# Splitting modulated tokens into two 12-bit parts once per tile and layer, and loading the parts

## The chip, the core and the metric

The kernel runs on one core of a Trainium2 chip. Its time is the device time of one execution in microseconds (us). Names: PE is the matrix engine (TensorE), ACT ScalarE, DVE VectorE, POOL GpSimd, SP the engine that issues most transfers; `L339` is line 339 of the kernel before. A tile is 128 tokens; there are 18 (16 of the latent grid, 2 of the context).

## The reference

Two layers of a hybrid block on 2048 latent tokens and 256 context tokens, 1024 features, fp32. In each layer all head groups read the same modulated input through one projection:

```python
h = x * (1.0 + scale[:, None]) + shift[:, None]          # and hc = ctx * (1 + scale_c) + shift_c
(aq, ak, av, ag, bq, bk, bv, bg, cq, ck, cv, cg, du, dg) = jnp.split(h @ w_in, IN_SPLITS, axis=-1)
ya = gqa(aq, ak, av)          # group A: 4 heads, 2 key heads, rms-normed q and k, rotary
yb = diff_attention(bq, bk, bv)   # group B: 4 heads, two softmax maps each
yc = neighbourhood(cq, ck, cv)    # group C: 4 heads, 8 x 16 window plus the context keys
yd = s5(du)                       # group D: state-space layer over the tokens
y = concat(ya * silu(ag), yb * silu(bg), yc * silu(cg), yd * silu(dg)) @ w_out
x = layer_norm(ALPHA * x + gate * y)
```

`w_in` has 3328 columns, so `h @ w_in` is done here in parts: eleven passes ("sweeps") over the 18 tiles in each layer, each for the columns of one unit of work.

## The kernel before

*Products in two parts.* A product of fp32 numbers is made of three products of numbers with 12-bit mantissas (type fp32r, which PE takes at full rate): the tile h is split into H and L, the weights into WH and WL, and `mm3k` adds H WH + H WL + L WH for each of the 8 feature tiles, 24 matmuls a tile of tokens. H is a copy of h into fp32r by ACT (L337), L = h - H by POOL (L339), or, where `solo` is set, a quarter by POOL and three quarters by DVE (L340).

*Where the split stands.* The modulated tokens of a layer lie in DRAM (`hT`, 512 KB a tile). Every sweep loads each tile from there (`load_h`, L390, issued by SP) and splits it again (`split`). In the first layer the first sweep, that of group D, makes h from the input (`modulate`) and stores it; for the second layer the output projection of the first does so in `late`, for one tile while the products of the next are made.

*Stages of a layer.* The sweep of group D's input; the state-space scan; a sweep for A's first unit together with group D's gates; then the chain of ten attention units, a0 b0 a1 b1 c0 b2 c1 b3 c2 c3, which takes most of the time; the output projection. The two first sweeps run by themselves (`sweep`). The other nine units' sweeps run beside the attention of units before them (`sweep_beside`), as five streams of pieces: `pe` (matmuls, a feature tile a piece), `act` and `dve` (what is done with the product), `load` (load and split), `keys` (transposes of keys). `attend_a` and `attend` are written out by hand: they call `F.pe`, `F.act`, `F.dve` at fixed places, and these emit the next piece of a stream whose condition holds. `load` goes two tiles ahead (`("mm", j - 2) in at`). `F.light` says whether the DVE may take a share of L; it is set in C units.

*What sets the order.* In the chain, PE, ACT and DVE run in the order in which the program emits. POOL's and SP's orders are laid out by a scheduler. Every engine works off its instructions in order, so one that waits holds what is queued behind it.

*In a B unit* a step has the scores of one map (L998), their maxima (L1042), the exponentials (L1057), the combination of two maps on DVE (L1081, 1024 and 1280 columns), transposes (L1097) and products with values (L1123). The sweep of a C unit beside it splits the keys on DVE (L736, L737). In an A unit DVE finds maxima (L810) and DVE and POOL add up sums (L894).

The lines about the split:

```python
def split(self, h, solo, later=None):
    H = self.hp.tile([128, NK, 128], F32R, name="hH", bufs=2)
    L = self.hp.tile([128, NK, 128], F32R, name="hL", bufs=2)
    nc.scalar.activation(H, h, AF.Copy)
    a = 2 if solo else NK
    nc.gpsimd.tensor_tensor(L[:, :a], h[:, :a], H[:, :a], op=OP.subtract)
```

Of the kernel before, what the change touches and what calls it, by code (L numbers as in the profile page):

```python
# [35 lines left out]
AHEAD = 8  # L36
A_HEAD = 1
# [19 lines left out]
class Beside:  # L57
    """Streams of pieces of work that run beside attention: a projection's products, what ScalarE and VectorE do
    with them, the operands, and the keys' transposes. A stream yields None after a piece, and a condition
    where the next piece needs another stream's."""  # L60
    def __init__(self, prev, per):
        self.prev, self.per, self.sub = prev, per, []
# [20 lines left out]
class Fill:  # L83
    """Projections beside attention, one after another: plan names them, and what makes their streams."""
    def __init__(self, plan):
        self.plan, self.made, self.last, self.freed = list(plan), {}, None, set()
        self.q, self.t, self.light, self.draining, self.merged = [], 0, False, False, False
# [10 lines left out]
    def release(self, name):  # L98
        """The place for a projection's results is free."""
# [16 lines left out]
    def dve(self):  # L116
        for s in self.q[:2]:
            while s.sub:
                s.sub.pop(0)()
# [32 lines left out]
    def ahead(self, name, n):  # L152
        """The first steps of the first projection."""
# [7 lines left out]
class Net:  # L161
# [9 lines left out]
    # ------------------------------------------------------------------ set-up  # L171
    def consts(self):
# [32 lines left out]
        self.hT = {(l, t): dr.tile([128, NK, 128], F32, name=f"hT{l}_{t}") for l in range(DEPTH) for t in range(NT)}  # L205
# [6 lines left out]
    def stage(self):  # L212
        """Six banks of PSUM for one stage of the work."""
# [22 lines left out]
    def ada_w(self, l, c, j, p, bufs):  # L236
        """Two feature tiles of 512 columns of the modulation's weights."""
        w = p.tile([128, 2, 512], F32, name="hT", bufs=bufs)
# [22 lines left out]
    def ada(self, l, p):  # L261
        """Shift and scale, features on partitions."""
# [8 lines left out]
    def ada_beside(self, prev, F, chunks):  # L271
        """The same in pieces that run beside attention, for chunks of a layer's columns each."""
# [4 lines left out]
        def fetch(i):  # L277
            if i < len(jobs):
                c, j = jobs[i]
                ws[i] = self.ada_w(*chunks[c], j, self.hp, 2)  # L280

        def pe():
            yield lambda: S.prev is None or S.prev.read
            fetch(0)
            fetch(1)
            for i, (c, j) in enumerate(jobs):
# [4 lines left out]
                for k in (2 * j, 2 * j + 1):  # L291
# [3 lines left out]
                    if k % 2:  # L295
                        fetch(i + 2)
                    yield None

        def act():
            for c in range(len(chunks)):  # L300
                yield lambda: c in pss and (c < 1 or c - 1 in done)
                rows[c] = self.ada_row(pss.pop(c), self.hp.tile([2, 512], F32, name="hH", bufs=2))
# [1697 lines left out]
```

## Time and profile before

| | before |
|---|---|
| time, median of 3 runs | 5335.41 us (5329.9 to 5342.77) |
| span of the profiled execution | 5332.0 us (no other time of it is shown) |
| PE busy | 4758.8 us, 89% |
| DVE busy | 3709.5 us, 70% |
| ACT busy | 2903.1 us, 54% |
| POOL busy | 2474.4 us, 46% |
| moved by DMA | 460.67 MB, mean 86 GB/s |
| mean granted PE clock | 0.953 |

Busy time is the union of an engine's instructions; matmuls are pipelined and their ends are modelled, so a busy PE can still have short waits inside. A wait is put down to the instruction whose end released it. The granted clock is a share of full speed (1.0 is 2.4 GHz, 0.5 is 1.2 GHz). Stretches used below: 70 to 196 us group D's sweep of the first layer, 2805 to 2891 us that of the second; 4017 to 4228 us unit b1 of the second layer; six C units (c0, c1, c2 of both layers).

### The profile page before, as it was taken

The page shows a single profiled execution, that of the slowest core. Times are in us where ns is not written, and L with a number is a line of the kernel's source. Part 1 is how long each engine was busy: PE and PEld are TensorE (multiplying, and loading weights), DVE is VectorE, ACT ScalarE, POOL GpSimd, SP SyncE. Part 2 cuts the span into 40 slices and gives each one's busy share as a digit, 9 for nine tenths or more (in the row PEclk, how much of TensorE's full clock was granted, in tenths as well). Part 3 has the DMA queues.
Part 4 walks back from the last instruction along what each step waited for, and adds up shares of the span by engine and source line. Part 5 has one row for each costly group of instructions (what it writes and reads, how often), then busy time and mean ns, then how long its engine had stood idle before and what let it go on. Part 6 is the DMA issues. An engine that isn't in the chain of part 4 may idle for free. (4 is left out here: it accounts for less than half of the span.)

```text
span 5332.0 us, 87066 instructions
## 1 busy us (share of the span) xinstructions
PE 4758.8 (89%) x31076; PEld 3619.3 (68%) x31076; DVE 3709.5 (70%) x7186; ACT 2903.1 (54%) x6882; POOL 2474.4 (46%) x3017
## 2 busy tenths in 40 slices
PE   7878988899899998998997889988998989989999
PEld 3776546665678777775677765476656777867777
DVE  8575758876785966933974847697768759578345
ACT  3432437644676876854333434476447768667541
POOL 5355544645445354441533745546554544544322
PEclk8999999999999999999998999999999989989999
DMA  7734101111113122134556261112111221221333
GB/s 246 213 110 129 40 27 36 60 44 34 53 55 93 51 75 72 46 106 125 179 185 189 92 169 45 32 36 59 44 42 52 60 83 47 82 63 52 96 120 114
DMA packets 360193, 460.67 MB, mean 86 GB/s; under 512 B 161872, under 2 KB 262224, under 8 KB 359760
## 3 DMA queue, kind: packets, MB, share of 16 engines
q1 hardware_dynamic: 353712, 449.80, 27.7%
q8 instruction: 246, 4.03, 0.3%
q10 hardware_dynamic: 6048, 5.31, 0.3%
q14 instruction: 187, 1.53, 0.1%
HBM read 363.48 MB, written 91.49 MB: 85 GB/s over the span
## 5 line engine op out<-in xcount | busy, mean ns | idle before, releaser
L339 POOL TENSOR_TENSOR hL<-hT,hH 128x1024 fp32r<-128x1024 f32 (+1 forms) x396 | 822.7, 2079 | 897.9 <-ACT hH L337 705.6
L380 PE MATMUL pj<-WH,hH 128*128 128x256 f32 (+2 forms) x2592 | 825.8, 319 | 11.5 <-ACT b_v L729 2.9
L382 PE MATMUL pj<-WH,hL 128*128 128x256 f32 (+2 forms) x2592 | 765.0, 295 | 32.1 <-POOL hL L339 32.1
L381 PE MATMUL pj<-WL,hH 128*128 128x256 f32 (+2 forms) x2592 | 761.5, 294 | 0.0
L380 PEld LDWEIGHTS pj<-WH,hH 128*128 128x128 f32 x2592 | 506.8, 196 | 121.4 <-issue 72.3
L1111 ACT ACTIVATE PT<-tr 128x512 f32<-128x512 f32 (+1 forms) x788 | 440.2, 559 | 209.4 <-PE tr L1097 200.6
L382 PEld LDWEIGHTS pj<-WH,hL 128*128 128x128 f32 x2592 | 506.0, 195 | 39.9 <-POOL hL L339 37.8
L381 PEld LDWEIGHTS pj<-WL,hH 128*128 128x128 f32 x2592 | 507.7, 196 | 23.9 <-issue 1.9
L878 ACT ACTIVATE PT<-sx 128x512 f32<-128x512 f32 x584 | 315.1, 592 | 359.4 <-PE sx L876 352.1
L337 ACT ACTIVATE hH<-hT 128x1024 fp32r<-128x1024 f32 x396 | 415.9, 1053 | 134.6 <-PE pj L381 57.6
L1057 ACT ACTIVATE Ta<-sx,sm 128x1024 f32<-128x1024 f32 (+1 forms) x340 | 324.0, 953 | 154.9 <-DVE sm L1051 145.6
L1042 DVE TENSOR_REDUCE sm<-sx 128x1 f32<-128x1024 f32 (+1 forms) x276 | 319.9, 1159 | 66.4 <-PE sx L998 65.1
L883 PE MATMUL acc<-PT,a_v 128*64 128x512 f32 (+1 forms) x1168 | 324.4, 633 | 0.0
L998 PE MATMUL sx<-b_kst,qs 128*128 128x512 f32 (+2 forms) x618 | 220.7, 445 | 113.4 <-ACT Ta L1057 113.2
L894 DVE TENSOR_TENSOR Ta<-Ta,PT 128x512 f32<-128x512 f32 x288 | 259.7, 942 | 71.7 <-ACT PT L878 71.4
L1081 DVE SCALAR_TENSOR_TENSOR Tb<-Tb,sm 128x1280 f32<-128x1280 f32 x128 | 300.2, 2346 | 0.0
L894 POOL TENSOR_TENSOR Ta<-Ta,PT 128x512 f32<-128x512 f32 x160 | 225.7, 1429 | 158.1 <-ACT PT L878 157.6
L340 DVE TENSOR_TENSOR hL<-hT,hH 128x768 fp32r<-128x768 f32 x161 | 178.1, 1107 | 167.6 <-ACT hH L337 167.1
L1123 PE MATMUL acc<-PT,b_v 128*64 128x128 f32 (+1 forms) x3200 | 278.7, 290 | 5.3 <-DVE yo L1153 2.5
L875 PE MATMUL sx<-Tb,a_kst 128*128 128x512 f32 x584 | 250.5, 429 | 19.5 <-ACT PT L878 19.5
L810 DVE TENSOR_REDUCE mxa<-sz 128x1 f32<-128x512 f32 x256 | 175.4, 685 | 132.8 <-PE sz L808 131.0
L810 DVE TENSOR_REDUCE mxa<-sy 128x1 f32<-128x1024 f32 (+1 forms) x256 | 209.5, 818 | 76.7 <-PE sy L808 73.7
(389 smaller groups left out, 12797.7 us busy)
## 6 DMA issues: line engine op xcount, KB each, us to landing
hT<-hT SPq DMA_DIRECT2D x396, 512.0 KB, 3.5
hT<-in_w_ada SPq DMA_DIRECT2D x48, 512.0 KB, 3.9
wst<-in_w_in SPq DMA_DIRECT2D x576, 32.0 KB, 1.8
yin<-y SPq DMA_DIRECT2D x30, 512.0 KB, 3.7
hT<-in_xT SPq DMA_DIRECT2D x18, 512.0 KB, 4.3
U<-ud SPq DMA_DIRECT2D x64, 144.0 KB, 3.5
x<-zn SPq DMA_DIRECT2D x18, 512.0 KB, 2.7
hT<-hn SPq DMA_DIRECT2D x18, 512.0 KB, 4.1
```

Source lines behind the costliest of these rows:

```text
L337: nc.scalar.activation(H, h, AF.Copy)
L339: nc.gpsimd.tensor_tensor(L[:, :a], h[:, :a], H[:, :a], op=OP.subtract)
L380: nc.tensor.matmul(ps, H[:, k, :], WH[k][:, c0:c1], start=(k == 0), stop=False)
L381: nc.tensor.matmul(ps, H[:, k, :], WL[k][:, c0:c1], start=False, stop=False)
L382: nc.tensor.matmul(ps, L[:, k, :], WH[k][:, c0:c1], start=False, stop=(k == NK - 1))
L810: nc.vector.tensor_reduce(nm if one else mx[:, j:j + 1], s, axis=AX.X, op=OP.max, negate=one)
L878: nc.scalar.activation(PTs[x][h][:, :w], o[:, h * 512:h * 512 + w], AF.Exp, scale=0.125)
L883: nc.tensor.matmul(acc[h * 64:(h + 1) * 64, :w], v[:, kts[x], :], PT[h][:, :w], start=(x == 0), stop=(x == n - 1))
L894: eng.tensor_tensor(sums[e][:, h, :w], first[:, :w], PT[h][:, :w], op=OP.add)
L1042: nc.vector.tensor_reduce(mx[:, j:j + 1] if len(tiles) > 1 else nm, s, axis=AX.X, op=OP.max, negate=len(tiles) == 1)
L1057: nc.scalar.activation(r["P"](a, b), src, AF.Exp, bias=r["sm"][:, 5:6], accum_out=r["sm"][:, 6 + j:7 + j])
L1111: nc.scalar.activation(PT[:w, x:y], tr[:w, x * 128:y * 128].rearrange("p (a b) -> p a b", b=128), AF.Copy)
```

## The change

The split is made once for each tile and layer, where the modulated tile is made: in the first sweep of the first layer (`make_h`), and in `late` of its output projection, there out of a tile `z` that is used again. Both parts go to DRAM as one tensor `hs` of 1 MB a tile, stored through SP as plain fp32. All other sweeps load both parts with one transfer (`load_h`) into a tile of type fp32r; that transfer is issued by GpSimd. There are three buffers for the parts (`HBUF`) instead of two each for h, H and L, and `load` goes three tiles ahead. The share of L goes by the `solo` rule everywhere (2 of 8 feature tiles on GpSimd), `F.light` and the deferred DVE piece (`S.sub`) are gone. The weights of the modulation (`ada_w`) use the same three buffers. In group A the product with the gains is made in place.

```diff
+HBUF = 3
-        self.hT = {(l, t): dr.tile([128, NK, 128], F32, name=f"hT{l}_{t}") for l in ... for t in ...}
+        self.hs = {(l, t): dr.tile([128, 2, NK, 128], F32, name=f"hs{l}_{t}") for l in ... for t in ...}
-    def split(self, h, solo, later=None):
-        H = self.hp.tile([128, NK, 128], F32R, name="hH", bufs=2)
-        L = self.hp.tile([128, NK, 128], F32R, name="hL", bufs=2)
-        nc.scalar.activation(H, h, AF.Copy)
-        a = 2 if solo else NK
-        nc.gpsimd.tensor_tensor(L[:, :a], h[:, :a], H[:, :a], op=OP.subtract)
-        rest = lambda: nc.vector.tensor_tensor(L[:, a:], h[:, a:], H[:, a:], op=OP.subtract)
-        if solo:
-            later.append(rest) if later is not None else rest()
-        return H, L
+    def split(self, h, hs):
+        nc.scalar.activation(hs[:, 0], h, AF.Copy)
+        a = 2
+        nc.gpsimd.tensor_tensor(hs[:, 1, :a], h[:, :a], hs[:, 0, :a], op=OP.subtract)
+        nc.vector.tensor_tensor(hs[:, 1, a:], h[:, a:], hs[:, 0, a:], op=OP.subtract)
+    def hs_tile(self):
+        return self.hp.tile([128, 2, NK, 128], F32R, name="hs", bufs=HBUF)
-    def load_h(self, l, t, first=False):
-        h = self.hp.tile([128, NK, 128], F32, name="hT", bufs=2)
-        self.nc.sync.dma_start(h, self.io["xT"][t] if first else self.hT[l, t])
-        return h
+    def load_h(self, l, t):
+        hs = self.hs_tile()
+        self.nc.gpsimd.dma_start(hs, self.hs[l, t])
+        return hs[:, 0], hs[:, 1]
+    def make_h(self, l, t, p):
+        h = p.tile([128, NK, 128], F32, name="h0")
+        self.nc.sync.dma_start(h, self.io["xT"][t])
+        self.modulate(l, t, h, [h[:, k, :] for k in range(NK)])
+        hs = self.hs_tile()
+        self.split(h, hs)
+        self.nc.sync.dma_start(self.hs[l, t], hs.bitcast(F32))
+        return hs[:, 0], hs[:, 1]
 # sweep
-            h = self.load_h(l, t, first)
-            if first:
-                self.modulate(l, t, h, [h[:, k, :] for k in range(NK)])
-                nc.sync.dma_start(self.hT[l, t], h)
-            H, L = self.split(h, solo)
+            H, L = self.make_h(l, t, make) if make else self.load_h(l, t)
 # sweep_beside
-                    yield lambda: n * per + i in split and not S.sub
+                    yield lambda: n * per + i in split
-                yield lambda: j < 2 or ("mm", j - 2) in at
-                split[j] = self.split(self.load_h(l, tiles[j][0]), F.light, S.sub)
+                yield lambda: j < HBUF or ("mm", j - HBUF) in at
+                split[j] = self.load_h(l, tiles[j][0])
 # proj_a
-            x = e.tile([128, 192], F32, name="xq")
-            nc.gpsimd.tensor_tensor(x[:, c0:], pe[:, c0:192], gain[:, c0:], op=OP.mult)
+            x = pe[:, 0:192]
+            nc.gpsimd.tensor_tensor(x[:, c0:], x[:, c0:], gain[:, c0:], op=OP.mult)
 # out_proj, late
-                    hT = p.tile([128, NK, 128], F32, name="hn")
+                    hs = p.tile([128, 2, NK, 128], F32R, name="hs")
-                    self.modulate(l + 1, t, hT, src)
-                    nc.sync.dma_start(self.hT[l + 1, t], hT)
+                    self.modulate(l + 1, t, h, src)      # h is z, viewed by feature tile
+                    self.split(h, hs)
+                    nc.sync.dma_start(self.hs[l + 1, t], hs.bitcast(F32))
```

On POOL in unit b1 of the second layer, the order before (hL are the subtractions, yms the norm's power, qn the queries' parts, pe the gate products):

```order
L339 TENSOR_TENSOR hL<-hT,hH 128x1024
L1145 TENSOR_SCALAR yms<-yms 128x1
L976 TENSOR_TENSOR qn<-b_q,one 128x4x32
L1146 TENSOR_TENSOR yms<-yms,mhalf 128x1
L976 TENSOR_TENSOR qn<-b_q,one 128x4x32
L977 TENSOR_TENSOR qn<-b_q,qn 128x4x32 x2
L537 TENSOR_TENSOR pe<-pe,half 128x2x64
L339 TENSOR_TENSOR hL<-hT,hH 128x1024
L1145 TENSOR_SCALAR yms<-yms 128x1
```

And the same place with the change (its line numbers are other ones):

```order
L388 DMA hs<-hs_7_118 128x2048
L1148 TENSOR_SCALAR yms<-yms 128x1
L979 TENSOR_TENSOR qn<-b_q,one 128x4x32
L1149 TENSOR_TENSOR yms<-yms,mhalf 128x1
L979 TENSOR_TENSOR qn<-b_q,one 128x4x32
L980 TENSOR_TENSOR qn<-b_q,qn 128x4x32 x2
L388 DMA hs<-hs_8_119 128x2048
L541 TENSOR_TENSOR pe<-pe,half 128x2x64
L1148 TENSOR_SCALAR yms<-yms 128x1
```

Each subtraction has given its place to a load's issue, and one of two now stands ahead of the gate product instead of behind it.

At the end of the first layer's output projection, the order on SP before has the loads of the next layer's first tiles (16, 17, 0, 1) among the transfers of the output projection's tiles 8 and 9 (x is the stored output, yin and xin its inputs):

```order
L390 DMA hT<-hT_16_127 128x1024
L1783 DMA yin<-y_12_177 128x1024
L1785 DMA xin<-in_xn 128x1024
L390 DMA hT<-hT_17_128 128x1024
L358 DMA wst<-in_w_in 128x256 x3
L1849 DMA hT_8_119<-hn 128x1024
L390 DMA hT<-hT_0_111 128x1024
L358 DMA wst<-in_w_in 128x256 x2
L390 DMA hT<-hT_1_112 128x1024
```

With the change they stand on POOL, there behind the split of the output projection's last tile:

```order
L336 TENSOR_TENSOR hs<-z,hs 128x256
L1835 TENSOR_TENSOR zn<-zn,lg 128x1024
L336 TENSOR_TENSOR hs<-z,hs 128x256
L388 DMA hs<-hs_16_127 128x2048
L388 DMA hs<-hs_17_128 128x2048
L388 DMA hs<-hs_0_111 128x2048
L388 DMA hs<-hs_1_112 128x2048
```

Four loads have moved from the output projection's ninth tile to behind its last.

## Rows read from the trace of the kernel before

**Rows 1.** groups by line of the whole run, columns as in part 5

```profile
L339 POOL TENSOR_TENSOR hL<-hT,hH 128x1024 fp32r<-128x1024 f32 (+1 forms) x396 | 822.7, 2079 | 897.9 <-ACT hH L337 705.6 <-DVE sm L1063 187.6 <-DVE kf L671 1.6
...
L337 ACT ACTIVATE hH<-hT 128x1024 fp32r<-128x1024 f32 x396 | 415.9, 1053 | 134.6 <-PE pj L381 57.6 <-PE s L381 26.6 <-issue 23.7
...
L340 DVE TENSOR_TENSOR hL<-hT,hH 128x768 fp32r<-128x768 f32 x161 | 178.1, 1107 | 167.6 <-ACT hH L337 167.1
```

**Rows 2.** waits of TensorE (PE), whole run: us, times, longest

```profile
PE sx L998 <- ACT Ta L1057: 113.2, 135, 4.9
PE pj L382 <- POOL hL L339: 32.1, 25, 2.7
...
PE s L380 <- ACT a_v L595: 21.8, 7, 6.9
...
PE sy L808 <- DVE mxa L810: 17.7, 24, 1.9
PE sz L808 <- DVE mxa L810: 17.7, 24, 1.7
...
PE s L382 <- POOL hL L339: 13.9, 13, 4.7
...
PE s L380 <- ACT hH L337: 10.1, 7, 4.6
```

**Rows 3.** busy time of each engine in three stretches (columns in its first line)

```profile
core 0: us, PE busy (x) PEld busy (x) DVE busy (x) ACT busy (x) POOL busy (x), PEclk, DMA share, GB/s
70.00:196.00 126.00, 104.49 (x609) 79.45 (x606) 94.35 (x257) 62.33 (x136) 66.95 (x64) 0.86 0.76 237
...
2805.00:2891.00 86.00, 66.23 (x494) 63.88 (x495) 42.31 (x115) 31.60 (x54) 31.51 (x26) 0.88 0.55 181
...
4017.00:4228.00 211.00, 189.16 (x1449) 148.42 (x1448) 187.29 (x289) 164.92 (x389) 92.01 (x112) 0.95 0.16 47
```

**Rows 4.** timeline of VectorE in a B unit: start, length, instruction

```profile
4103.44 3.67 DVE L1081 SCALAR_TENSOR_TENSOR Tb<-Tb,sm 128x1280 f32<-128x1280 f32 x1
...
4116.59 2.40 DVE L736 CAST ks<-pe 128x128 fp32r<-128x128 f32 x1
...
4127.43 3.66 DVE L1081 SCALAR_TENSOR_TENSOR Tb<-Tb,sm 128x1280 f32<-128x1280 f32 x1
```

**Rows 5.** timeline of GpSimd in the same window

```profile
4103.38 2.38 POOL L339 TENSOR_TENSOR hL<-hT,hH 128x1024 fp32r<-128x1024 f32 x1 [5.86 <-DVE sm L1063]
...
4116.31 2.59 POOL L339 TENSOR_TENSOR hL<-hT,hH 128x1024 fp32r<-128x1024 f32 x1 [1.26 <-ACT hH L337]
```

**Rows 6.** timeline of VectorE at the end of that unit

```profile
4199.41 1.53 DVE L1081 SCALAR_TENSOR_TENSOR Tb<-Tb,sm 128x1280 f32<-128x1280 f32 x1
...
4210.55 1.53 DVE L1081 SCALAR_TENSOR_TENSOR Tb<-Tb,sm 128x1280 f32<-128x1280 f32 x1
4212.00 0.42 DVE L736 CAST ks<-pe 128x128 fp32r<-128x128 f32 x1
```

**Rows 7.** waits of TensorE, 70 to 196 us

```profile
PE s L382 <- POOL hL L339: 10.6, 8, 4.7
PE s L380 <- ACT hH L337: 4.2, 4, 2.2
```

**Rows 8.** waits of TensorE, 2805 to 2891 us

```profile
PE s L380 <- ACT hH L337: 5.8, 3, 4.6
PE s L382 <- POOL hL L339: 2.6, 4, 1.1
```

**Rows 9.** DMA issues: out<-in, queue, count, KB each, median us to landing

```profile
hT<-hT SPq DMA_DIRECT2D x396, 512.0 KB, 3.5
...
bm<-coutm SPq DMA_DIRECT2D x10, 512.0 KB, 6.2
```

**Rows 10.** timeline of SP: start, us on the queue, issue

```profile
2808.93 0.32 SPq L1849 DMA_DIRECT2D hT<-hn  x1
```

**Rows 11.** copies of L337 in the six C units, summed

```profile
sum 664.00, ACT 95.24; mean ACT 15.87
```

More of the change, by code (lines that the diff above doesn't have):

```diff
@@ L61, in __init__ @@
     def __init__(self, prev, per):
-        self.prev, self.per, self.sub = prev, per, []
+        self.prev, self.per = prev, per
         self.free, self.w, self.mm, self.read, self.keys = False, False, False, False, False
@@ L86, in __init__ @@
         self.plan, self.made, self.last, self.freed = list(plan), {}, None, set()
-        self.q, self.t, self.light, self.draining, self.merged = [], 0, False, False, False
+        self.q, self.t, self.draining, self.merged = [], 0, False, False
     def fetch(self):
@@ L116, in dve @@
     def dve(self):
-        for s in self.q[:2]:
-            while s.sub:
-                s.sub.pop(0)()
         self.go(2)
@@ L204, in consts @@
         dr = self.dram
-        self.hT = {(l, t): dr.tile([128, NK, 128], F32, name=f"hT{l}_{t}") for l in range(DEPTH) for t in range(NT)}
+        self.hs = {(l, t): dr.tile([128, 2, NK, 128], F32, name=f"hs{l}_{t}") for l in range(DEPTH) for t in range(NT)}
         self.x1 = {t: dr.tile([128, D], F32, name=f"x1_{t}") for t in range(NT)}
@@ L236, in ada_w @@
     def ada_w(self, l, c, j, p, bufs):
-        w = p.tile([128, 2, 512], F32, name="hT", bufs=bufs)
+        w = p.tile([128, 2, 512], F32, name="hs", bufs=bufs)
         src = self.io["w_ada"][l].rearrange("(k p) n -> p k n", p=128)
@@ L279, in fetch @@
                 c, j = jobs[i]
-                ws[i] = self.ada_w(*chunks[c], j, self.hp, 2)
+                ws[i] = self.ada_w(*chunks[c], j, self.hp, HBUF)
         def pe():
             yield lambda: S.prev is None or S.prev.read
-            fetch(0)
-            fetch(1)
+            for i in range(HBUF):
+                fetch(i)
             for i, (c, j) in enumerate(jobs):
@@ L295, in pe @@
                     if k % 2:
-                        fetch(i + 2)
+                        fetch(i + HBUF)
                     yield None
@@ L301, in act @@
                 yield lambda: c in pss and (c < 1 or c - 1 in done)
-                rows[c] = self.ada_row(pss.pop(c), self.hp.tile([2, 512], F32, name="hH", bufs=2))
+                rows[c] = self.ada_row(pss.pop(c), self.ap.tile([2, 512], F32, name="row", bufs=1))
                 yield None
@@ L386, in sweep_tiles, with sweep @@
         return [(t, c) for t, c in ts if c[1] > c[0]]
-    def load_h(self, l, t, first=False):
-        h = self.hp.tile([128, NK, 128], F32, name="hT", bufs=2)
-        self.nc.sync.dma_start(h, self.io["xT"][t] if first else self.hT[l, t])
-        return h
-    def sweep(self, l, parts, first=False, solo=False):
+    def load_h(self, l, t):
[10 more added lines that the diff above has]
+        return hs[:, 0], hs[:, 1]
+    def sweep(self, l, parts, make=None):
         nc = self.nc
@@ L853, in beat @@
             return True
-        F.light = False
         yield True
@@ L1179, in attend @@
             if maps == 2:
-                F.light = False
                 at(i - 2, pv, 1)
@@ L1256, in attend @@
             else:
-                F.light = True
                 if i == 0:
@@ L1526, in epi @@
                 nc.vector.tensor_copy(uT[i][:, :, c0:c0 + 8], src)
-        self.sweep(l, [([(2816, 256)], (0, 256), (0, 256), epi, None, None)], first=(l == 0), solo=True)
+        with ExitStack() as es:
+            self.sweep(l, [([(2816, 256)], (0, 256), (0, 256), epi, None, None)],
+                       self.pool(es, "h0", bufs=2) if l == 0 else None)
         for g in range(NG):
@@ L1837, in out_proj, with late @@
                 nc.sync.dma_start(self.x1[t], zn)
-                def late(t=t, zn=zn):
-                    hT = p.tile([128, NK, 128], F32, name="hn")
+                def late(t=t, zn=zn, h=z.rearrange("p (k n) -> p k n", k=NK)):
+                    hs = p.tile([128, 2, NK, 128], F32R, name="hs")
                     src = []
@@ L1898, in run @@
                         begin()
-                        self.sweep(l, [*others, (segs, cols, ctx_cols, epi, None, self.nc.gpsimd)], solo=True)
+                        self.sweep(l, [*others, (segs, cols, ctx_cols, epi, None, self.nc.gpsimd)])
                     return run
```

## The prediction

> **What bounds the kernel now.** I read the groups by line first [rows 1]: the split that the change takes out of the sweeps costs ScalarE 415.9 us (L337), GpSimd 822.7 us (L339) and VectorE 178.1 us (L340) per run, 396 times each but for L340 (161). Neither engine's sum is the span, so the next view is who TensorE waits for [rows 2]. The largest wait is that of the scores of group B for the exponentials (113.2 us, L998 for L1057). The split itself is waited for directly in three rows: 32.1 and 13.9 us for hL, 10.1 us for hH. The other rows of the group are first-sweep and group A waits for ScalarE's copies and VectorE's maxima. The busy times by stretch [rows 3] show where there is room: in a B unit (4017 to 4228 us) PE is busy 189.16 of 211 us and DVE 187.29, both near full, at a granted clock of 0.95; in the first sweep (70 to 196 us) the DMA engines are 0.76 busy, in the second layer's first sweep (2805 to 2891 us) 0.55.
>
> The timeline of that B unit tells why DVE is full. DVE's L1081 on 1280 columns takes 3.67 and 3.66 us at 4103.44 and 4127.43, and a cast of 128 columns (L736) takes 2.40 us [rows 4]; GpSimd's subtraction of 1024 columns runs at 4103.38 and at 4116.31 [rows 5], that is, together with the first and the last of these. At the end of the unit, where no subtraction runs, the same instructions take 1.53 us (twice) and 0.42 us [rows 6]. So per two tiles of queries DVE loses 2.14 + 1.98 = 4.1 us to being held while GpSimd subtracts, and this unit's DVE is what the exponentials wait for.
>
> **The change part by part.** *Split gone from the sweeps.* 396 splits become 36 (18 in the first sweep, 18 in the first output projection): by the means of [rows 1] ScalarE loses 360 x 1.05 = 379 us, GpSimd some 770 us, VectorE about 140 us of own work. This is worth time only where TensorE waits:
> - Direct waits: 32.1 + 13.9 + 10.1 = 56.1 us. The 10.6 + 4.2 us of the first sweep stay, since that sweep still splits [rows 7]; the 5.8 + 2.6 us of the second layer's first sweep turn into a wait for a load, counted below [rows 8]. That leaves 33 us. Bounds 0 (each wait is taken by a load) and 56; I take 33.
> - B units beside C projections (six): two tiles take 4127.43 - 4103.44 = 23.99 us, 12.0 each; the undisturbed tile takes 4210.55 - 4199.41 = 11.14 us, with slightly less projection in it. So 0 to 0.86 us a tile. PE's own work lies close under this, so I take 0.5, for some 14 tiles a unit while a projection runs: 84 x 0.5 = 42 us (0 to 72). The two B units beside A projections at the same rate: 28 x 0.5 = 14 us (0 to 24).
> - A units: TensorE waits 17.7 + 17.7 = 35.4 us for maxima that VectorE finds late [rows 2]; VectorE's sums and rotations stand behind the same subtractions. I take 26 (0 to 35).
> - The a0 sweeps: 21.8 us of waiting for ScalarE's copy of values [rows 2]; with 1.05 us less on ScalarE and as much on VectorE per tile I take 12 (0 to 22).
>
> Sum of gains: 33 + 42 + 14 + 26 + 12 = 127 us.
>
> *Split moved into the output projection of the first layer.* Per tile 1.05 us of ScalarE, 1.11 us of VectorE, some of GpSimd. PE is the busy engine there, with VectorE in second place; costed at nothing as long as VectorE keeps up (18 x 1.1 = 20 us if it did not). At its end it does cost: before, the first tiles of the next sweep were loaded long ahead on SP; now the order puts them on GpSimd behind the last tile's split. That is 1.05 + 1.11 us of split and one load before TensorE can start. A 0.5 MB load lands 3.5 us after its issue (median), another kind of 0.5 MB load 6.2 us [rows 9]; 1 MB is then between 3.5 and 12.4 us, and I take 7.0, twice the row of the same tile. So 9 us, rounded to 10 for the modulation ahead of it (0 to 20).
>
> *Stores of twice the size.* In the first sweep 18 x 0.5 MB = 9.4 MB more are written in 126 us, 75 GB/s. The stretch moves 237 GB/s at a share of 0.76 [rows 3], so a full share would be 312 GB/s, just these 75 more. The stores are not waited for at once; I take 5 us (0 to 20).
>
> *Loads of twice the size, issued by GpSimd.* 378 issues. What GpSimd spends on one is in no row: SP's issue of such a transfer takes 0.32 us [rows 10], and the dearest reading is that it holds GpSimd and VectorE as long as the subtraction did (2.59 us at most in [rows 5]), in which case the gains beyond the direct waits vanish. I take the issue row as the nearer one, with 5 us for loads that come late at a unit's start. A load waits for the products of the tile three before; queued behind it on GpSimd stand the gate products and the powers of group B's norm, and VectorE waits for those. The products lie two tiles back, about 24 us in a B unit, so the wait is over when GpSimd comes to it. SP loses 396 issues.
>
> The Trainium skill (SBUF — State Buffer, section "SBUF: two separate sides") speaks against this step: it says that a DMA issued by GpSimd has its descriptors written by GpSimd's cores, which a VectorE copy in a two-port mode locks out, 620 ns becoming 3100 ns. No run here shows it. By it each load could be 2.5 us later, which the two tiles' lead hides except in the second layer's first sweep, where with three in flight an estimate is 18 x 2.5 / 3 = 15 us more. The same skill (DMA: Bandwidth & Descriptors, "Measured (HBM→SBUF, 128 partitions, SWDGE, issued from GpSimd)") has 6.15 us for 1 MB; by that figure my 10 us would be 9.
>
> *Small parts.* A's product by the gains is made in place, which adds no instruction; the modulation's weights get a third buffer. Nothing is counted for either.
>
> Sum: 127 - 10 - 5 - 5 = 107 us. The profiled span is 5332.0 us; nothing else is shown of that execution, and the median of the timed runs is 3.4 us above it. 5332 - 107 + 3 = 5228 us.
>
> **The rivals.**
> 1. *TensorE is the bound and the freed engines only idle more.* For it: 189.16 of 211 us busy in the B unit. Against: 22 us of room in that unit alone, and the undisturbed tile. Then only the direct waits go: 33 - 20 = 13 us, 5322 us.
> 2. *The loads become the bound: slower.* Place: the second layer's first sweep, which takes a tile each 86 / 18 = 4.8 us [rows 3], and the six C units, where 664 us hold 95.24 / 1.05 = 91 tiles [rows 11], 7.3 us each. If 1 MB, with the change of type, lands every X us with three in flight, the price is 18 (X - 4.8) + 91 (X - 7.3). It eats the 127 - 10 us of the other terms at X = 8.0. At X = 10 it is 339 us: 5332 - 117 + 339 + 3 = 5557 us. For it: a 0.5 MB load of 6.2 us. Against: the 3.5 us of the tile's own loads, and that transfers overlap.
> 3. *All terms at their upper bound, and some clock back*: of the three stretches of [rows 3] the one in which PE is busy for the largest share has the highest granted clock, 0.95 against 0.86 and 0.88 (1.0 is 2.4 GHz, the lower level 1.2 GHz). 56 + 72 + 24 + 35 + 22 = 209, less 20, is 189 us: 5332 - 189 + 3 = 5146 us. The clock would come on top and is not counted.
>
> **How the numbers follow.** Forecast 0.53, its own range 5170 to 5290. Rival 1 0.18, rival 2 0.14, rival 3 0.15. About 0.2% (11 us) is what a measurement tells from no change. Of rival 1, 0.12 is still faster, 0.05 the same and 0.01 slower; with the others that is faster 0.80, same 0.05, slower 0.15. The range 5115 to 5360 leaves out the strong form of rival 2 and little of rival 3.
>
> **What would show it.** Right: L1081 on 1280 columns near 1.53 us and L736 near 0.4 us throughout; two tiles of a B unit in about 23 us; no TensorE wait of several us for hs loads in A and B units; ScalarE's and GpSimd's sums down by about 380 and 400 to 770 us. Wrong: loads that land after 12 us or more, TensorE waiting for hs in C units, or the same 3.67 us on VectorE beside a load's issue. The prediction fails as a whole if the loads' interval passes 8 us.

## The result and the profile after

The changed kernel takes 5159.16 us (median; 5156.56 to 5163.03) against 5335.18 us (5329.9 to 5342.77) before: ratio 0.9676, 95% interval 0.9661 to 0.9691, 176 us faster. The forecast was 5228 us with a range of 5115 to 5360. The profiled span is 5156.9 us, 175.1 us less than before.

The page's first part, busy us of each engine (share of the span) and instructions:

```profile
PE 4681.1 (91%) x31076; PEld 3585.3 (70%) x31076; DVE 3215.5 (62%) x7061; ACT 2568.4 (50%) x6522; POOL 1912.5 (37%) x3035
```

TensorE runs the same 31076 matmuls. Of the 175.1 us, 77.7 are less busy time of TensorE (4758.8 before), so its idle time fell by 97.4 us. ScalarE lost 335 us, VectorE 494 and GpSimd 562. The prediction took some 140 us of own work off VectorE; the other 350 us or so mean that instructions that stayed became shorter, and the lines below show which.

Two groups by line, columns as in [rows 1]: the loads' issues on GpSimd, and the combination of two maps on VectorE:

```profile
L388 POOL DMA_DIRECT2D hs<-hs x378 | 227.7, 603 | 956.0 <-PE pj L379 475.6 <-PE s L379 158.5 <-PE sz L1001 54.4
...
L1084 DVE SCALAR_TENSOR_TENSOR Tb<-Tb,sm 128x1280 f32<-128x1280 f32 x128 | 200.3, 1565 | 0.0
```

The combination before:

```profile
L1081 DVE SCALAR_TENSOR_TENSOR Tb<-Tb,sm 128x1280 f32<-128x1280 f32 x128 | 300.2, 2346 | 0.0
```

An issue takes 0.60 us of GpSimd, and 378 of them 227.7 us. The 1280-column combination takes 1.57 us on average, against 2.35 before. By the trace 49 of the 128 took over 2 us before (two of them in [rows 4]); now 3 do.

TensorE's waits, columns as in [rows 2]:

```profile
PE sx L1001 <- ACT Ta L1060: 57.4, 51, 4.4
PE s L377 <- DMA hs<-hs: 23.7, 3, 20.3
PE d L1661 <- DMA U<-ud: 19.8, 2, 10.4
...
PE d L1732 <- DVE big L1721: 19.0, 2, 11.8
PE d L1661 <- DMA bm<-binm: 15.9, 7, 4.8
...
PE pj L242 <- DMA hs<-in_w_ada: 15.1, 7, 10.6
PE s L377 <- ACT a_v L599: 14.9, 7, 5.0
PE s L379 <- POOL hs L336: 14.0, 10, 3.0
...
PE sy L812 <- DVE mxa L814: 8.6, 17, 1.1
...
PE s L377 <- ACT hs L334: 5.7, 5, 2.8
...
PE sz L812 <- DVE mxa L814: 2.8, 9, 0.4
```

Of the kernel before, the three rows of the scan (its loads U and bm, and VectorE's `big` at its end):

```profile
PE d L1658 <- DMA U<-ud: 13.2, 2, 7.1
PE d L1658 <- DMA bm<-binm: 12.7, 8, 2.5
...
PE d L1729 <- DVE big L1718: 7.8, 1, 7.8
```

The wait for the exponentials is halved (113.2 before), that for maxima is 8.6 + 2.8 instead of 35.4. Of the waits for the split the first sweep's are left (14.0 + 5.7). New is one wait of 20.3 us within the 23.7 us for a load of the parts: the start of the second layer. The scan's three waits grew from 33.7 to 54.7 us.

The same B unit as in [rows 4 to 6], VectorE and then GpSimd:

```profile
3960.79 1.53 DVE L1084 SCALAR_TENSOR_TENSOR Tb<-Tb,sm 128x1280 f32<-128x1280 f32 x1
3962.24 0.22 DVE L740 CAST ks<-pe 128x128 fp32r<-128x128 f32 x1
...
3983.10 1.54 DVE L1084 SCALAR_TENSOR_TENSOR Tb<-Tb,sm 128x1280 f32<-128x1280 f32 x1
```

```profile
3969.87 0.62 POOL L388 DMA_DIRECT2D hs<-hs  x1 [3.46 <-PE pj L379]
```

Two tiles now take 3983.10 - 3960.79 = 22.31 us (23.99 before); the combination takes 1.53 us and the cast of L740 (L736 before) 0.22 us. Where the subtraction stood there is an issue of 0.62 us.

Busy times by stretch, columns as in [rows 3]: of the kernel before the start of group D's scan with its loads U and bm (196 to 250 us), unit a0 and unit b1 of the first layer, then of the changed kernel the same three and the second layer's first sweep:

```profile
196.00:250.00 54.00, 38.24 (x368) 34.92 (x368) 21.73 (x76) 16.15 (x44) 16.41 (x23) 0.87 0.83 227
487.00:805.00 318.00, 281.54 (x1341) 172.53 (x1341) 219.79 (x356) 124.53 (x248) 160.06 (x167) 0.95 0.12 40
1370.00:1593.00 223.00, 202.87 (x1567) 160.60 (x1566) 189.54 (x302) 174.50 (x418) 93.61 (x115) 0.96 0.15 49
```

```profile
202.00:265.00 63.00, 42.86 (x368) 39.16 (x367) 23.64 (x94) 14.28 (x41) 15.11 (x25) 0.86 0.84 257
493.00:781.00 288.00, 270.94 (x1343) 166.75 (x1343) 193.93 (x356) 107.98 (x230) 126.00 (x166) 0.99 0.22 73
1324.00:1528.00 204.00, 192.13 (x1569) 155.29 (x1569) 162.25 (x303) 158.36 (x400) 60.76 (x115) 0.99 0.30 98
2723.00:2807.00 84.00, 61.78 (x495) 60.76 (x496) 19.72 (x87) 11.72 (x29) 16.91 (x28) 0.85 0.97 332
```

Unit a0 went from 318 to 288 us. TensorE's busy time fell with it, 281.54 to 270.94 us, while the granted clock rose from 0.95 to 0.99: 281.54 x 0.95 = 267.5 and 270.94 x 0.99 = 268.2, the same work. The scan's start went the other way, 54 to 63 us, and the second layer's first sweep now fills the DMA engines (share 0.97, 332 GB/s).

Stage lengths in us, worked out from the traces by cutting each run's one profiled execution at the same matmuls of TensorE, counted from the start (both layers added; e2 to e12 are the experiments below):

| stages | before | after | e2 | e3 | e4 | e9 | e10 | e11 | e12 |
|---|---|---|---|---|---|---|---|---|---|
| group D's first sweep, layer 1 | 126 | 131 | 131 | 115 | 131 | 131 | 132 | 134 | 123 |
| start and end of group D's scan (before and after the a0 sweep) | 198 | 236 | 236 | 187 | 215 | 245 | 241 | 209 | 218 |
| a0 sweeps | 374 | 338 | 328 | 351 | 335 | 337 | 339 | 334 | 333 |
| A units | 1244 | 1151 | 1152 | 1155 | 1149 | 1178 | 1171 | 1152 | 1149 |
| b0 | 484 | 481 | 481 | 470 | 478 | 488 | 487 | 478 | 476 |
| b1, b2, b3 | 1357 | 1257 | 1284 | 1299 | 1248 | 1291 | 1307 | 1252 | 1248 |
| C units | 863 | 855 | 861 | 885 | 853 | 859 | 963 | 857 | 852 |
| output projection 1 and first sweep, layer 2 | 391 | 408 | 408 | 377 | 414 | 408 | 412 | 406 | 401 |
| rest | 296 | 300 | 299 | 297 | 299 | 299 | 301 | 300 | 299 |

From before to after, the gains are 93 us in A units, 100 in b1 to b3, 36 in the a0 sweeps, 8 in C units and 3 in b0: 240 us. The costs are 5 in the first sweep, 38 around the scan, 18 at the layer's change and 4 elsewhere: 65 us.

The scan's start, the a0 sweep and the scan's end lie one after the other, and their sum is 572 us before and 574 after: a gain and a cost that cancel. e3, without the subtraction and with loads of 0.5 MB, has 538 us there, and e11, the changed kernel with such loads, 543. e2 (564) and e9 (582) differ there from the changed kernel although their edits leave these stages alone, so a difference of up to some 10 us in this sum has no meaning.

### The profile page after: what moved, and what is told of

It reads as the page before. It is cut to its first block, busy times and chain, and to the rows that moved or that the text cites. A ratio compares the mean times of both kernels' runs of the same rounds, so it can differ in the third digit from the quotient of the medians.

```text
span 5156.9 us, 85866 instructions
## 1 busy us (share of the span) xinstructions
PE 4681.1 (91%) x31076; PEld 3585.3 (70%) x31076; DVE 3215.5 (62%) x7061; ACT 2568.4 (50%) x6522; POOL 1912.5 (37%) x3035
## 5 line engine op out<-in xcount | busy, mean ns | idle before, releaser
L377 PE MATMUL pj<-WH,hs 128*128 128x256 f32 (+2 forms) x2592 | 814.9, 314 | 22.1 <-ACT b_v L733 7.1
L378 PE MATMUL pj<-WL,hs 128*128 128x256 f32 (+2 forms) x2592 | 753.3, 291 | 2.7 <-POOL WL L367 2.7
L379 PE MATMUL pj<-WH,hs 128*128 128x256 f32 (+2 forms) x2592 | 752.3, 290 | 0.0
L377 PEld LDWEIGHTS pj<-WH,hs 128*128 128x128 f32 x2592 | 498.1, 192 | 125.3 <-issue 68.2
L388 POOL DMA_DIRECT2D hs<-hs x378 | 227.7, 603 | 956.0 <-PE pj L379 475.6
L378 PEld LDWEIGHTS pj<-WL,hs 128*128 128x128 f32 x2592 | 499.2, 193 | 26.6 <-POOL WL L367 3.3
L379 PEld LDWEIGHTS pj<-WH,hs 128*128 128x128 f32 x2592 | 497.7, 192 | 2.4 <-issue 2.4
L1001 PE MATMUL sx<-b_kst,qs 128*128 128x512 f32 (+2 forms) x618 | 218.3, 441 | 58.1 <-ACT Ta L1060 57.4
L897 DVE TENSOR_TENSOR Ta<-Ta,PT 128x512 f32<-128x512 f32 x288 | 217.0, 794 | 77.0 <-ACT PT L881 76.5
L1100 PE MATMUL tr<-ident,Ta 128*128 128x128 f32 x1576 | 246.5, 278 | 13.9 <-ACT PT L1114 10.2
L1045 DVE TENSOR_REDUCE sm<-sy 128x1 f32<-128x768 f32 (+1 forms) x260 | 245.4, 944 | 15.7 <-PE sy L1001 14.4
L377 PE MATMUL s<-WH,hs 128*128 128x256 f32 (+1 forms) x576 | 193.4, 337 | 44.9 <-DMA hs<-hs 20.7
```

The costliest lines, as they stand in the source:

```text
L377: nc.tensor.matmul(ps, H[:, k, :], WH[k][:, c0:c1], start=(k == 0), stop=False)
L378: nc.tensor.matmul(ps, H[:, k, :], WL[k][:, c0:c1], start=False, stop=False)
L379: nc.tensor.matmul(ps, L[:, k, :], WH[k][:, c0:c1], start=False, stop=(k == NK - 1))
L897: eng.tensor_tensor(sums[e][:, h, :w], first[:, :w], PT[h][:, :w], op=OP.add)
L1001: nc.tensor.matmul(s[:, o0:o0 + w], lt, r["ks"][:, k0:k0 + w], start=(x == 0), stop=(x == len(r["ops"]) - 1))
L1045: nc.vector.tensor_reduce(mx[:, j:j + 1] if len(tiles) > 1 else nm, s, axis=AX.X, op=OP.max, negate=len(tiles) == 1)
```

## The experiments

Theory A: GpSimd's subtraction and VectorE hold each other up, and its end is the gain. Theory B, its rival: the gain is the own time of copy and subtraction and the waits for their results. Theory Q, another rival: the subtraction delayed what was queued behind it on GpSimd, above all the norms' powers and the gate products. C (three buffers let loads come earlier) and M (the place of a buffer in SBUF) come up once each. Ratios are to the kernel before on the same chip.

**e1: GpSimd's time put back.** One tile `xd` (its own lines are left out) and one instruction in the changed kernel's `load`:

```diff
                 split[j] = self.load_h(l, tiles[j][0])
+                if self.xd is not None:
+                    self.nc.gpsimd.tensor_tensor(self.xd, self.xd, self.xd, op=OP.subtract)
```

> The changed kernel with one more GpSimd subtraction (128x864 of a scratch tile, nobody reads it, it waits for nothing) right behind each load's issue in the nine sweeps that run beside attention, some 300 in all. Theory A (GpSimd's two-input operations and VectorE's hold each other up, and that was what the subtraction cost): VectorE's 1280-column combination goes from 1.56 us mean back to 2.5 us or more, its busy time rises by 150 to 300 us, and 80 to 150 us of time come back: 5240 to 5310 us. Theory B (the gain is the subtraction's and copy's own time and the waits for their results): GpSimd is 37% busy and nobody waits for the scratch, so no more than 15 us: 5159 to 5175 us.

5363.86 us, ratio 1.0064 (1.0045 to 1.0084): slower than expected by either theory, about 205 us over the changed kernel. The busy time of this tile's instructions in two stretches, b0 and a1 (us, VectorE, GpSimd and their number):

```profile
814.00:1122.00 308.00, 0.00 (x0) 148.82 (x87) 0.85 0.21 67
1122.00:1420.00 298.00, 0.00 (x0) 0.00 (x0) 0.99 0.26 83
```

Since the subtraction waits for nothing, the scheduler let it run ahead: 87 of its 316 stand in the first layer's b0, none in a1. Only a0 and b0 became slower (a0 by 34 and 28 us in the two layers, b0 by 67 and 68). VectorE's busy time rose by 251 us, as theory A had it, but its 1280-column combination only to 1.62 us on average, not to 2.5. So GpSimd's time can cost as much as the change gained, but this run doesn't price it at the places where it had been.

**e2: ScalarE's time put back.**

```diff
+                if self.xd is not None:
+                    self.nc.scalar.activation(self.xd, self.xd, AF.Copy)
```

> The changed kernel with one more ScalarE copy (128x864 of a scratch tile, nobody reads it) at each load in the nine sweeps beside attention, some 300 of 0.9 us, 270 us of ScalarE in all. Theory A (hold-up of VectorE by GpSimd): ScalarE has room (50% busy), 0 to 25 us slower: 5159 to 5185 us. Theory B (own time of the engines: ScalarE's copy stood ahead of the exponentials that TensorE waits for): at least 60 us slower, 5220 us or more.

5181.89 us, ratio 0.9722 (0.9706 to 0.9738), 23 us over the changed kernel, at the upper end of what theory A expects. b1 to b3 take 26 us more (1257 to 1284), C units 6 more and the a0 sweeps 9 less; A units and b0 don't notice 0.9 us of ScalarE a tile.

**e3: the kernel before without the subtraction.**

```diff
         nc.scalar.activation(H, h, AF.Copy)
-        a = 2 if solo else NK
-        nc.gpsimd.tensor_tensor(L[:, :a], h[:, :a], H[:, :a], op=OP.subtract)
-        rest = lambda: nc.vector.tensor_tensor(L[:, a:], h[:, a:], H[:, a:], op=OP.subtract)
...
-        return H, L
+        return H, H
```

> The kernel before without the subtraction: H stands for L in the products, so the result is another one; ScalarE's copy, the loads of 0.5 MB on SP and two buffers stay. Theory A: all of the gain in the attention units (some 240 us in the changed kernel) but ScalarE's part comes, and none of the costs of storing and loading both parts (some 65 us): 5080 to 5150 us. Theory B (own times and waits of copy and subtraction alike, shared over three engines): the waits for hL, 46 us, and about half of the rest: 5220 to 5290 us. Theory C (the gain is from loads that come earlier, three buffers): 5280 us or more.

5135.07 us, ratio 0.9633 (0.9616 to 0.965), as theory A expects, and C is out: two buffers and SP's loads of 0.5 MB stayed. In A and B units GpSimd alone made L, so there it is GpSimd's subtraction that went; in C units and in the sweeps that run by themselves VectorE's share (L340) went with it. A units need 1155 us, what they need in the changed kernel. In b1 to b3 the subtraction's end brings 58 of 100 us; with the copy's 26 us of e2 most of the rest is found. TensorE's wait for the exponentials says the same, between 113.2 and 57.4 us:

```profile
PE sx L992 <- ACT Ta L1051: 69.1, 86, 4.4
```

**e4: loads issued by SP.**

```diff
-        self.nc.gpsimd.dma_start(hs, self.hs[l, t])
+        self.nc.sync.dma_start(hs.bitcast(F32), self.hs[l, t])
```

> The changed kernel with its loads issued by SP as plain fp32 (the tile seen as fp32), instead of by GpSimd. If the second layer's late start (PE waits 20 us for its first load) is the place of the first loads behind the last split in GpSimd's order, and each issue's 0.6 us on GpSimd costs a little: 5159 - 15 to - 35 = 5124 to 5144 us. If the doubled bytes are what makes that start and the scan's loads late: 5150 to 5165 us. If SP's queue is the worse place (loads that wait for products hold the output projection's and the weights' transfers): 5175 us or more.

5123.11 us, ratio 0.9616 (0.9602 to 0.963), 36 us below the changed kernel, but not where it was expected: the layer's change is no shorter (414 us for 408); the scan's stages are (236 to 215), and b1 to b3 (1257 to 1248).

**e5 and e6: subtraction or copy, spread over the units.** As e1, with an operand that was loaded; e6 has `tensor_copy(self.xd, old...)` in its place.

```diff
+                if self.xd is not None and j:
+                    self.nc.gpsimd.tensor_tensor(self.xd, old.rearrange("p k n -> p (k n)")[:, :864], self.xd,
+                                                 op=OP.subtract)
+                old = split[j][0]
```

> As e1, but each added GpSimd subtraction (128x864) reads the parts loaded one tile earlier, so it can't run ahead as in e1, where nearly all of them ran in a0 and b0: 292 of 1.7 us or more, spread over the units. Theory A (hold-up by two-input operations): VectorE's 1280-column combination and 128x512 sums are again stretched where they meet it, VectorE's busy time up by 100 to 250 us, A units and B units beside C projections slower, together 70 to 150 us: 5230 to 5310 us. Theory B (own time and direct waits only): up to 30 us: 5160 to 5190 us.

> As e5 with a GpSimd copy of the same 864 columns (one input) in place of the subtraction (two inputs). If what costs time is the time on GpSimd's queue, ahead of the norms' and gates' operations, it costs as much per us of GpSimd as e5. If it is the meeting of two-input operations on GpSimd with VectorE's (theory A), VectorE's busy time rises by under 60 us and the run stays within 30 us of the changed kernel, 5150 to 5190 us, well below e5.

e5: 5236.83 us, ratio 0.9829 (0.9809 to 0.9849). e6: 5194.49 us, 0.9758 (0.9737 to 0.9779). The added group of e5 and of e6, columns as in [rows 1]:

```profile
L472 POOL TENSOR_TENSOR xd<-hs,xd 128x864 f32<-128x864 f32 x300 | 627.8, 2093 | 486.6 <-DMA hs<-hs 481.1 <-DVE sm L1081 4.2
```

```profile
L472 POOL COPY xd<-hs 128x864 f32<-128x864 f32 x300 | 283.4, 945 | 467.5 <-DMA hs<-hs 463.5 <-DVE sm L1048 3.6
```

Both waited for the landing of a load that was issued just ahead, which the edit was not meant to add. By spans, e5 costs 5233.8 - 5156.9 = 76.9 us for 627.8 us of GpSimd, 0.12 us per us, e6 29.0 us for 283.4, 0.10. The equal price is the outcome of "time on GpSimd's queue". But VectorE's busy time rose by 204.5 us in e5 and by 53.5 in e6, e5's time lies in theory A's range and e6's just above it. The two runs don't decide.

**e9 and e10: the same time in two copies.** The operand is that of two tiles earlier. The lines are e9's; e10 has `tensor_copy(self.xd, old[j - 2])` twice for the subtraction.

```diff
+            old = []
...
+                old.append(split[j][0].rearrange("p k n -> p (k n)")[:, :864])
+                if self.xd is not None and j > 1:
+                    self.nc.gpsimd.tensor_tensor(self.xd, old[j - 2], self.xd, op=OP.subtract)
```

> As e5, but the added GpSimd subtraction reads the parts loaded two tiles earlier, so that GpSimd doesn't wait for a landing with it. Some 280 of 2.05 us, 570 us of GpSimd. Theory A (hold-up by two-input operations): VectorE's busy time up by 100 to 200 us over the changed kernel, 50 to 90 us slower: 5210 to 5250 us. Theory Q (time on GpSimd's queue, ahead of norms and gates): the same time as e10.

> As e9 with two GpSimd copies (one input each) of the same 864 columns in place of each subtraction, about 0.95 us each, so that GpSimd is busy about as long (some 530 us more). Theory A: no hold-up, VectorE's busy time up by under 70 us, and at least 25 us faster than e9: 5170 to 5200 us. Theory Q: within 12 us of e9.

e9: 5231.46 us, ratio 0.9817 (0.9803 to 0.983), with VectorE 199 us busier, both in theory A's ranges. e10: 5351.02 us, 1.0037 (1.0024 to 1.005): neither theory's figure, and VectorE's busy time rose by 131 us where theory A wanted under 70. GpSimd's wait for a landing was still there (e9's group, 474.5 us). e10's added groups, TensorE's wait that only e10 has, and one meeting of GpSimd and VectorE in its b0:

```profile
L474 POOL TENSOR_TENSOR xd<-hs,xd 128x864 f32<-128x864 f32 x284 | 591.5, 2083 | 474.5 <-DMA hs<-hs 473.1
```

```profile
L475 POOL COPY xd<-hs 128x864 f32<-128x864 f32 x568 | 536.0, 944 | 301.6 <-DMA hs<-hs 288.0 <-DVE sm L1050 6.1 <-DMA wst<-in_w_in 2.5
```

```profile
PE pj L377 <- DMA hs<-hs: 73.0, 33, 6.5
```

```profile
833.90 0.90 POOL L475 COPY xd<-hs 128x864 f32<-128x864 f32 x1
```

```profile
833.92 2.22 DVE L1089 SCALAR_TENSOR_TENSOR Tb<-Tb,sm 128x1280 f32<-128x1280 f32 x1
```

First, 108 us of e10 lie in the C units (855 to 963): a load there is issued behind copies, and TensorE waits 73.0 us for loads in projections. That is rival 2's place, reached by holding the issue. Second, the meeting: beside a copy that began 0.02 us earlier and took 0.90 us, VectorE's 1.53 us became 2.22; 24 of the 128 combinations were held like this one. A GpSimd operation with one input holds VectorE up too, so the pair e9 and e10 can't tell A from Q. The Trainium skill (SBUF — State Buffer, section "SBUF: two separate sides") says this: a VectorE operation with two inputs in SBUF and any GpSimd operation that reads SBUF exclude each other for a whole instruction. The trace agrees to some 0.2 us: VectorE took 0.69 us longer where 0.88 us of copy were left, and 2.14 us longer where 2.32 us of subtraction were left in [rows 4, 5].

**e7 and e8: the late start of the second layer.** One buffer fewer where the output projection makes the parts; e8 is e7 with e4.

```diff
-                    hs = p.tile([128, 2, NK, 128], F32R, name="hs")
+                    hs = p.tile([128, 2, NK, 128], F32R, name="hs", bufs=1)
```

> The changed kernel with one buffer instead of two for the parts made in the output projection (8 KB per partition less). The third buffer of the loaded parts then no longer lies where that tile lay, and in GpSimd's order the first three loads of the second layer come ahead of the output projection's later tiles instead of behind its last. Theory M (memory placement makes the late start of the second layer): TensorE's 20.3 us wait for its first load goes, 10 to 20 us faster than the changed kernel: 5139 to 5150 us. If the start is late because of the last tile's chain or the doubled bytes: 5155 to 5165 us.

> e4 (loads issued by SP) and e7 (one buffer for the output projection's parts) together. If both gains are separate places: 36 us from e4 and 10 to 20 us from e7, 5103 to 5113 us. If e4's gain was at the same place: 5120 us.

e7: 5162.67 us, ratio 0.9698 (0.9677 to 0.9718), no gain. GpSimd at the layer's change in the changed kernel (start, length, instruction, idle before and what ended it):

```profile
2732.19 1.50 POOL L336 TENSOR_TENSOR hs<-z,hs 128x256 fp32r<-128x256 f32 x1 [10.21 <-ACT hs L334]
2738.80 1.77 POOL L388 DMA_DIRECT2D hs<-hs  x3 [5.11 <-DMA hs<-hs]
```

The load waits there 5.11 us for a store of the parts, although tile 16's own parts were stored long before: its buffer lies where the output projection's parts lie, and with one of those fewer, in e7, it is issued earlier (at 2626 us instead of 2739). TensorE's waits in that sweep of e7 are these alone:

```profile
PE pj L1523 <- DVE big L1570: 6.2, 1, 6.2
PE pj L1523 <- ACT ks L1519: 4.4, 3, 3.3
```

The 20.3 us wait is gone and the sweep is 7 us shorter (83.5 to 76.7), as theory M has it; but the scan's stages and the a0 sweeps after it take 8 us more (236.0 to 239.2, 337.6 to 342.3). That is no more than e9 takes there without such an edit, so whether the earlier start causes it is open. e8: 5119.51 us, 0.9612 (0.9594 to 0.963), not to be told from e4.

**e11: half the loaded bytes.**

```diff
-        self.nc.gpsimd.dma_start(hs, self.hs[l, t])
-        return hs[:, 0], hs[:, 1]
+        self.nc.gpsimd.dma_start(hs[:, 0], self.hs[l, t][:, 0])
+        return hs[:, 0], hs[:, 0]
```

> The changed kernel with loads of H alone (0.5 MB, GpSimd-issued) and H used for L too, so the result is another one; the stores stay at 1 MB. If the doubled loads are what makes the second layer's first sweep, the gates' sweeps and the rest of group D's scan later (they grew by 7, 9, 11, 11 and 7 us), most of it comes back: 5159 - 25 to - 45 = 5114 to 5134 us. If the issues on GpSimd or the memory placement do it: 5145 to 5165 us.

5126.51 us, ratio 0.9618 (0.9605 to 0.9632), 33 us below the changed kernel. Of the 38 us around the scan 27 come back (236 to 209), with the same 378 issues on GpSimd. Landing times (least, median, most) of the changed kernel's loads and of e11's:

```profile
DMA to landing us min/median/max: 5.0/5.2/11.9
```

```profile
DMA to landing us min/median/max: 3.7/4.0/9.9
```

**e12: a better version.** e8 with L made by VectorE alone:

```diff
-        a = 2
-        nc.gpsimd.tensor_tensor(hs[:, 1, :a], h[:, :a], hs[:, 0, :a], op=OP.subtract)
-        nc.vector.tensor_tensor(hs[:, 1, a:], h[:, a:], hs[:, 0, a:], op=OP.subtract)
+        nc.vector.tensor_tensor(hs[:, 1], h, hs[:, 0], op=OP.subtract)
```

> e8 (loads on SP, one buffer in the output projection) with the whole of L made by VectorE where the split is made, nothing by GpSimd. TensorE's 13 us of waiting for GpSimd's share in the first sweep goes, VectorE's 1024 columns take about 0.3 us more than 768: 5 to 15 us faster than e8, 5104 to 5114 us. If VectorE is the limit of the first sweep or of the output projection: 5120 us or more.

5099.53 us, ratio 0.9569 (0.9556 to 0.9582), the fastest version here, 60 us below the changed kernel; the interval lies below e8's. By spans it is 12.2 us below e8 (5110.6 to 5098.4), as expected, and 7.5 of these are the first sweep (130.1 to 122.6). The reason given there does not hold: of the wait for GpSimd (13.1 us in e8) nothing is left, but most of it became waits for ScalarE's copy (6.1 us in e8) and for VectorE's subtraction:

```profile
PE s L375 <- ACT hs L334: 10.5, 9, 2.0
...
PE s L377 <- DVE hs L335: 7.3, 9, 2.3
```

What did change in that sweep is the granted clock, 0.83 in e8 and 0.91 in e12; why it is higher is open.

## Why the prediction was right, and which terms were not

*Direct waits, 33 us.* The three rows of 56.1 us became 14.0 + 5.7: 36.4 us, of which the prediction books 8.4 as a load's wait. On its own count that is 28 us against 33, because the first sweep's waits grew from 14.8 to 19.7 us. Right in the main.

*B units, 42 + 14 us.* TensorE's wait for the exponentials fell by 113.2 - 57.4 = 55.8 us, the sum of the two terms. The place was not quite as told: b0 beside A's projection gained 3 us, not 14. There TensorE had little left to gain, as a stretch in the middle of the first layer's b0 before shows: it was busy for 47.57 of 50 us at the full clock, though VectorE, held up there too (a combination at 931 us takes 3.70 us), was fuller still (49.38):

```profile
925.00:975.00 50.00, 47.57 (x354) 37.91 (x351) 49.38 (x84) 42.61 (x108) 29.17 (x38) 1.00 0.13 40
```

*A units, 26 us.* The waits for maxima fell from 35.4 to 11.4 us, 24 us. *The a0 sweeps, 12 us:* the wait for ScalarE's copy fell from 21.8 to 14.9, 7 us. With these the waits that the prediction named fell by 123 us against its 127. They do not cover all that was gained in those stages: the a0 sweeps are 36 us shorter.

*The clock, priced at nothing.* The step that failed is that a gain is "worth time only where TensorE waits", together with rival 3's "The clock would come on top and is not counted." TensorE's busy time fell by 77.7 us for the same matmuls. In a0 all of it is the clock (0.95 to 0.99, the two products above); in b1 of the first layer 202.87 x 0.96 = 194.8 us of full-clock work became 192.13 x 0.99 = 190.2, so some 6 of 10.7 us. Counted over the whole traces, with the granted clock at each matmul, 387 us of TensorE's busy time lay at 1.2 GHz before and 299 after. Work that fills these 88 us at 1.2 GHz needs 44 at 2.4, so 44 of the 77.7 us are the clock: 30 us in A units, 20 in b1 to b3, less 6 elsewhere. The other 34 us lie inside matmuls whose ends are modelled, as short waits that no row names.

*Stores, 5 us:* the first sweep grew by 5.2, but that the figure fits is luck. No row has TensorE wait there for a transfer; its waits for the split grew by 4.9 us, and e12 takes 7.5 us off with the same stores. *The late start, 10 us:* 18 us, with a wait of 20.3. The prediction put it down to GpSimd's order behind the last split; e7 shows a shared place in SBUF, of which that order is the result, and that ending the wait alone gains nothing.

*Loads, 5 us.* This term was mis-sized, 38 us around the scan. It looked at units' starts, and the load interval never passed its 8 us there (84 / 18 = 4.7 us a tile in the second layer's first sweep). What it missed is who else loads then: group D's scan, whose stretch before had a DMA share of 0.83 already. With half the bytes (e11) 27 of these 38 us are gone, and 31 of the 574 us with the sweep in between. e4, at full bytes but from SP, gives back 21 (24 with the sweep), so the issuing engine has a part too; the two overlap, and how they divide is open. TensorE's own waits for the scan's loads grew by 9.8 us only, and its wait for VectorE at the scan's end by 11.2; why that one grew is not shown.

One reading behind this term does not hold. The prediction has the wait for the products over "when GpSimd comes to it"; in fact GpSimd idles 956.0 us ahead of its 378 issues, 475.6 of them for products of projections. Little hangs on it in the B units, as the chain below shows, and e4, which takes the issues off GpSimd, is 9 us shorter in b1 to b3.

So the net came out at 175 us by spans instead of 107, with two errors against each other: the gains were 240 us for 127, the costs 65 for 20. Of the 113 us that the gains are above the forecast, 89 are less busy time of TensorE in the stages that gained (in the others it rose by 11), the rest are waits that the prediction did not name. About 30 us on either side stand in the a0 sweeps and the scan around them, where they cancel.

*The mechanism.* That the subtraction's end is the main gain is shown by e3 (5332.0 - 5137.0 = 195 us by spans, with stores and loads as before), and ScalarE's share by e2. That VectorE is held up is shown at single instructions (3.67 against 1.53 us, 49 of 128 before and 3 after). Whether this hold-up or the time on GpSimd's queue costs the time, e5, e6, e9 and e10 don't tell: with e10's C units left out (194.7 - 107.8 = 86.9 us for 536.0 us of GpSimd) all four cost 0.10 to 0.16 us per us of GpSimd's time, whatever the operation; e1, whose added time is crowded into a0 and b0, cost 0.37 (202.2 us for 544.1). All of the four also held GpSimd at a landing.

The two kernels' own traces tell it for the B units. The chain that ended last, followed back step by step to what released each instruction or stood before it on its engine, runs like this through the two tiles of [rows 4] (shares of 30 us by line, the row ends where the view cuts it, then two of its pieces: start, length, instruction):

```profile
by line: DVE sm L1042 36.2%; DVE Tb L1081 28.7%; DVE ks L736 7.8%; issue 5.2%; ACT Ta L1057 4.0%; PE sy L998 3.7%; PE sx L998 2.4%; DVE sm L1051 2.4%; DVE yo L1153 1.6%; PE tr L1097 1.4%; DVE sm L1070 1.3%; DVE sm L1074 1.0%; DVE ks L737 1.
...
4103.53 3.58 DVE Tb L1081
...
4116.67 2.33 DVE ks L736
```

And with the change, through the same place (3959 to 3987 us):

```profile
by line: PE acc L1126 24.9%; PE tr L1100 20.6%; PE sx L1001 11.8%; PE pj L377 10.2%; PE pj L378 8.1%; PE sy L1001 8.0%; PE pj L379 8.0%; PE sz L1001 4.2%; PE acc L1137 2.4%; PE tr L989 1.7%; PE tr L747 0.8%
```

Before, the chain lay on VectorE, and both stretched instructions stand in it at nearly their full length; GpSimd does not stand in it. Now it lies on TensorE, which is why two tiles became shorter by 1.7 us and not by the 4.1 us of hold-up. Followed back from the end of each of b1 to b3 in both layers, VectorE has 761 of 1357 us of the chain before and 80 of 1257 after. GpSimd has 40 and 16; of the 40, 18 are the subtraction itself, and some 12 the norms' powers and the queries' parts queued behind it. In e5, e9 and e10 GpSimd has 57 to 108 us, most of it the added operation and what is queued behind it. So in these units the hold-up is what cost the time, and the added operations cost theirs in part in another way. In A units VectorE's part of the chain fell from 256 to 120 us and GpSimd's from 43 to 26; there both had a share, and how large each is remains open.

*The rivals.* Rival 1 (TensorE the bound) comes near only in b0; in the other units TensorE became the bound with the change. Rival 2 (loads) did not decide: 5.2 us a landing, the C units' sum no longer than before, and no row in which a projection beside attention waits for a load; e10 shows what it looks like where one does. The Trainium skill's rule that a VectorE copy can keep GpSimd from writing a DMA's descriptors (SBUF — State Buffer, section "SBUF: two separate sides") is not seen here: half of the 378 loads land within 5.2 us of their issue, where the fastest takes 5.0, and the issue itself takes GpSimd 603 ns on average; 48 loads take over 6 us, and what delays those is not shown. Rival 3 (5146 us) was nearest to the measured time, but not by its terms: the waits moved as the forecast had them, and of what came on top less than half is the clock that rival 3 mentioned and left out.

## What to carry to other kernels

Repeated preparation that sits on an otherwise idle engine is not free: look at the same instruction's length with and without it beside it, and take it out once if its result can be kept. When waits of a busy TensorE go, count the granted clock as a term of its own. To tell which of two delayed engines costs the time, follow the chain that ended last through the place itself: an operation added as a probe can cost the same time in another way. When loads double, look first at the stretch whose DMA share is already high, even if it is not the one that the loads are for; and ask whether an added buffer lies where the stage before still works.

## What was not expected of the hardware

A GpSimd copy with one input holds a VectorE operation with two inputs, as a subtraction does (2.22 against 1.53 us beside 0.90 us). An issue of a 1 MB load costs GpSimd 0.60 us, about twice SP's 0.32 us for the same load in e4. Halving a load's bytes shortens its landing only from 5.2 to 4.0 us (medians).
